# LoRA add on one core: the two-tile part of the output stored in four uneven pieces from two queues

## The chip, the cores and the metric

The kernel runs on one core of one Trainium2 chip. The metric is the device time of one execution in microseconds; lower is better. The core has a matmul engine (PE; its weight loads are shown apart as PEld), VectorE (DVE), ScalarE (ACT), GpSimd (POOL) and SyncE (SP). Data moves between HBM and the on-chip memory by 16 DMA engines, which all queues share. SyncE issues every transfer of the kernel before.

## The reference

```
x: (16, 512, 768) float32    A: (768, 16)    B: (16, 768)    scale: 0.5
lora = np.matmul(np.matmul(x, A), B)
return (x + scale * lora).astype(np.float32)
```

Flattened, x has 8192 rows of 768 numbers, 25.17 MB. As much is written, so 50.3 MB cross the DMA engines at least once.

## The kernel before

The 8192 rows are 64 tiles of 128 rows. All of x stays in one on-chip buffer `xs`, 128 partitions by 64 tiles by 768 numbers, and the result is added in place there, so a store reads what a load wrote.

Loads and stores go in parts, with a layout of their own: in a part of n tiles, partition p holds n consecutive rows of x. One partition's share of a part is therefore one run of n x 3072 bytes in HBM, and a DMA packet of the profile is one such run. `PARTS` (line 14) lists parts of 2, 6, 8, 16, 16 and 16 tiles; `LOADS` splits the first part of 16 into two loads of 8. A transfer of a part has 128 partition rows, 8 for each of the 16 DMA engines: 6,144 bytes a row for two tiles, 24,576 for eight, 49,152 for sixteen.

SyncE issues in this order: the loads of 2 and 6 tiles, A (24 rows of 2,048 bytes), B (16 rows of 3,072 bytes), the other loads, and then the stores in the order `STORES = [2, 1, 0, 3, 4, 5]`: the parts of 8, 6 and 2 tiles, then three of 16. Ahead of a store it waits on the semaphore `added`, on which VectorE counts finished parts (line 158). All this stands in one queue, and each DMA engine works off its share of that queue in order. The two-tile part is part 0, the third store.

The computing goes by chunks of four tiles. VectorE and ScalarE cast x to fp16 (`narrowed`, lines 99 and 101), the PE transposes it (line 193), ScalarE copies the transposed block out (line 143), the PE multiplies by A (line 201), ScalarE scales (line 147), the PE multiplies by B (line 212), and VectorE adds the result to `xs` (`summed`, line 154). The PE's program is a loop (`Fori`) over the chunks; the other engines' programs are unrolled.

GpSimd zeroes a scratch area and builds the identity matrix in the first two microseconds, and then waits at line 132 until `stored` has counted all six stores (16 each). That wait is the last thing it does before the closing barriers, and it is what keeps the kernel open until the output has landed. A wait is carried by the next instruction of its engine, here the branch out of the block that the loop ends.

Of the kernel before, what the change touches and what calls it, by code (L numbers as in the profile page):

```python
# [13 lines left out]
PARTS = [2, 6, 8, 16, 16, 16]  # L14
LOADS = [2, 6, 8, 8, 8, 16, 16]
STORES = [2, 1, 0, 3, 4, 5]

CHUNK = 4

# [2 lines left out]
def kernel(  # L22
# [8 lines left out]
    nc = tc.nc  # L31
    fp32 = mybir.dt.float32
    add = mybir.AluOpType.add
    P = 128

    x2 = x.flatten_outer_dims()
    out2 = out.flatten_outer_dims()
# [8 lines left out]
    NB = D // 32  # L46
    assert D % W == 0 and sum(LOADS) == NT == sum(PARTS) and sorted(STORES) == list(range(len(PARTS)))
    n_splits = [(n0, min(512, D - n0)) for n0 in range(0, D, 512)]
# [5 lines left out]
    xs = sb.tile([P, NT, D], fp32, name="xs")  # L54
# [17 lines left out]
    starts = [sum(PARTS[:i]) for i in range(len(PARTS))]  # L72

    def rows(t2, t0, n):
        i = max(i for i in range(len(PARTS)) if starts[i] <= t0)
        part = t2[ds(starts[i] * P, PARTS[i] * P), :].rearrange("(p s) d -> p s d", s=PARTS[i])
        return part[:, ds(t0 - starts[i], n), :]

    with tc.tile_critical():  # L79
        names = "zeroed ident a b a_t prep fed0 fed1 fed2 turned got proj y lora freed added".split()  # L80
        S = {k: nc.alloc_semaphore(name=f"s_{k}") for k in names}
        landed = [nc.alloc_semaphore(name=f"s_load{i}") for i in range(len(LOADS))]
        stored = nc.alloc_semaphore(name="s_stored")
        part_of = [i for i, n in enumerate(LOADS) for _ in range(n)]

        def load(i):
            t0, n = sum(LOADS[:i]), LOADS[i]
            nc.sync.dma_start(out=xs[:, t0 : t0 + n, :], in_=rows(x2, t0, n)).then_inc(landed[i], 16)
# [3 lines left out]
        def narrowed(engine, c, u):  # L92
# [16 lines left out]
            out=ident, in_=ident, compare_op=mybir.AluOpType.not_equal, fill=1.0,  # L109
# [8 lines left out]
            out=a_rows[0:NB, :, :], in_=A.rearrange("(b a) r -> b a r", a=32)  # L118
# [3 lines left out]
            load(i)  # L122
        nc.sync.wait_ge(S["prep"], 1)
        load(len(LOADS) - 1)
        summed_parts = 0
        for i in STORES:
            t0, n = starts[i], PARTS[i]
            if i + 1 > summed_parts:
                summed_parts = i + 1
                nc.sync.wait_ge(S["added"], summed_parts)  # L130
            nc.sync.dma_start(
                out=rows(out2, t0, n), in_=xs[:, t0 : t0 + n, :]
            ).then_inc(stored, 16)
        nc.gpsimd.wait_ge(stored, 16 * len(STORES))


        nc.scalar.wait_ge(S["ident"], 1)
# [2 lines left out]
        for c in range(NC):  # L140
# [3 lines left out]
            if c + 1 < NC:  # L144
# [3 lines left out]
                out=yt, in_=yt_ps, func=mybir.ActivationFunctionType.Copy, scale=sc  # L148
# [89 lines left out]
            expanded(s)  # L238


# [1 line left out]
_INS = ['x', 'A', 'B', 'scale']  # L242
_OUTS = [((16, 512, 768), 'float32')]
# [30 lines left out]
```

## Time and profile before

| | |
|---|---|
| median of 3 runs | 125.21 us (125.16 to 125.56) |
| the profiled execution's own time | 125.21 us |
| its span, first to last instruction | 123.4 us |
| PE / VectorE / ScalarE / GpSimd busy | 83.9 / 80.3 / 76.5 / 1.2 us |
| bytes moved | 50.45 MB at 409 GB/s |
| last store issued (SP) | 102.65 us |

The span leaves 1.8 us of the execution's time outside. The page cuts the span in 40 slices and gives a digit for each engine in each (its busy share in tenths); it also counts the DMA packets by size. Each transfer ends, on each DMA engine that it used, with one small packet of 4 bytes that counts up the transfer's semaphore. The kernel has no other packets under 512 bytes, so such a packet in a window of time tells that one engine has come to the end of its share of one transfer.

### The profile page before, as it was taken

Reading aid. Unit: us, or ns where it says so; the run is one execution under the profiler, and the core shown is the slowest. Engines: PE = TensorE matmul, PEld = TensorE weight load, DVE = VectorE, ACT = ScalarE, POOL = GpSimd, SP = SyncE. Lnnn points to the kernel's source line nnn. Section 1 sums busy time; section 2 is a strip of 40 time slices with the busy share of each in tenths; the row PEclk is TensorE's granted clock in tenths of the full one; section 3 lists DMA queues with packets and bytes.
Section 4 is the critical chain, followed back from the end, with each engine's and each line's share of the span. In section 5 each row is a group of like instructions: output and inputs, shape, how many; then the busy total and the mean of one; then the engine's idle time right before and its main releaser. Section 6 shows DMA issues by size and latency. Waiting matters only on the chain. (4 is left out here: it accounts for less than half of the span.)

```text
span 123.4 us, 1795 instructions
## 1 busy us (share of the span) xinstructions
PE 83.9 (68%) x608; PEld 39.2 (32%) x608; DVE 80.3 (65%) x102; ACT 76.5 (62%) x130; POOL 1.2 (1%) x7
## 2 busy tenths in 40 slices
PE   0000499999999999999999999999999770000000
PEld 0000343445444454444444444444444200000000
DVE  0002932999999999999999999989997592000000
ACT  4002539889898898988989889898898400000000
POOL 3000000000000000000000000000000000000000
PEclk9999999999999999999999999999999955555555
DMA  3999999999999799989799999989989989997960
GB/s 86 444 460 372 438 398 470 406 406 486 398 510 478 303 496 494 430 353 494 271 462 406 414 460 500 466 350 478 446 350 478 478 382 414 494 462 335 494 287 0
DMA packets 1942, 50.45 MB, mean 409 GB/s; under 512 B 236, under 2 KB 236, under 8 KB 532
## 3 DMA queue, kind: packets, MB, share of 16 engines
q1 hardware_dynamic: 1940, 50.43, 95.9%
q14 instruction: 2, 0.02, 0.0%
HBM read 25.26 MB, written 25.17 MB: 409 GB/s over the span
## 5 line engine op out<-in xcount | busy, mean ns | idle before, releaser
L154 DVE TENSOR_TENSOR xs<-xs,lo_ps 128x768 f32<-128x768 f32 x64 | 58.2, 950 | 5.9 <-PE lo_ps L212 5.1
L143 ACT CAST xt<-xt_ps 128x512 f16<-128x512 f32 x96 | 52.4, 577 | 10.5 <-PE xt_ps L193 8.8
L193 PE MATMUL xt_ps<-ident,xh 128*128 128x128 f16 x384 | 33.8, 226 | 12.3 <-PEq L186 12.3
L201 PE MATMUL yt_ps<-xt,a_mm 128*16 128x512 f16 x96 | 32.6, 395 | 1.6 <-PEq L186 1.6
L101 DVE CAST xh<-xs 128x1024 f16<-128x1024 f32 x32 | 21.9, 688 | 16.4 <-DMA xs<-in_x_dram 11.5
L193 PEld LDWEIGHTS xt_ps<-ident,xh 128*128 128x128 f16 x384 | 22.5, 100 | 30.4 <-issue 30.4
L212 PE MATMUL lo_ps<-b_mm,yt 16*128 16x512 f16 (+1 forms) x128 | 27.2, 331 | 3.7 <-PEq L186 1.6
L99 ACT CAST xh<-xs 128x1024 f16<-128x1024 f32 x16 | 16.8, 1048 | 9.1 <-DMA xs<-in_x_dram 9.1
L212 PEld LDWEIGHTS lo_ps<-b_mm,yt 16*128 16x128 f16 x128 | 9.6, 92 | 13.6 <-issue 7.6
L201 PEld LDWEIGHTS yt_ps<-xt,a_mm 128*16 128x16 f16 x96 | 7.1, 86 | 17.7 <-issue 12.7
L147 ACT ACTIVATE yt<-yt_ps 16x512 f16<-16x512 f32 x16 | 9.4, 587 | 0.9 <-PE yt_ps L201 0.9
L138 ACT ACT_TABLE_LOAD x1 | 1.3, 1283 | 0.9 <-SPq L79 0.9
L166 DVE STREAM_TRANSPOSE xs<-xs 32x512 f32<-32x512 f32 x1 | 1.0, 1027 | 0.0
L170 DVE CAST a_mm<-xs 32x96 f16<-32x96 f32 x4 | 0.9, 231 | 0.1
L172 DVE CAST b_mm<-xs 16x768 f16<-16x768 f32 x1 | 0.5, 549 | 0.0
L105 POOL MEMSET xs<- 32x512 f32 x1 | 0.5, 514 | 0.5 <-SPq L79 0.5
L108 POOL TENSOR_SCALAR_AFFINE_SELECT ident<-ident 128x128 f16<-128x128 f16 x1 | 0.3, 294 | 0.2 <-POOL ident L106 0.2
L138 ACT COPY first<-ident 128x1 f16<-128x1 f16 x1 | 0.2, 193 | 0.0
L106 POOL MEMSET ident<- 128x128 f16 x1 | 0.2, 194 | 0.0
L255 POOL MEMSET const-uint8-127<- 128x1 uint8 x1 | 0.1, 103 | 0.0
L255 POOL MEMSET const-bfloat16-1.0<- 128x1 bf16 x1 | 0.1, 102 | 0.0
L255 POOL MEMSET const-float32-0.0<- 128x1 f32 x1 | 0.1, 99 | 0.2 <-issue 0.2
(1 smaller groups left out, 0.1 us busy)
## 6 DMA issues: line engine op xcount, KB each, us to landing
out_dram<-xs SPq DMA_DIRECT2D x3, 6144.0 KB, 25.2
xs<-in_x_dram SPq DMA_DIRECT2D x2, 6144.0 KB, 45.9
xs<-in_x_dram SPq DMA_DIRECT2D x3, 3072.0 KB, 22.8
out_dram<-xs SPq DMA_DIRECT2D x1, 3072.0 KB, 29.3
xs<-in_x_dram SPq DMA_DIRECT2D x1, 2304.0 KB, 10.0
out_dram<-xs SPq DMA_DIRECT2D x1, 2304.0 KB, 34.4
xs<-in_x_dram SPq DMA_DIRECT2D x1, 768.0 KB, 4.5
out_dram<-xs SPq DMA_DIRECT2D x1, 768.0 KB, 35.7
```

The lines of the kernel that those rows point to most:

```text
L99: i = engine.copy(out=xh[u], in_=src)
L101: i = engine.tensor_copy(out=xh[u], in_=src)
L105: nc.gpsimd.memset(a_rows, 0.0).then_inc(S["zeroed"], 1)
L138: nc.scalar.copy(out=first, in_=ident[:, 0:1])
L143: nc.scalar.copy(out=xt[j], in_=xt_ps[j % NX]).then_inc(S["got"], 1)
L147: nc.scalar.activation(out=yt, in_=yt_ps, func=mybir.ActivationFunctionType.Copy, scale=sc).then_inc(S["y"], 1)
L154: nc.vector.tensor_tensor(out=xs[:, k, :], in0=xs[:, k, :], in1=lo_ps[k % 2], op=add).then_inc(S["freed"], 1)
L166: nc.vector.transpose(out=a_t, in_=a_rows.rearrange("b a r -> b r a")).then_inc(S["a_t"], 1)
L170: nc.vector.tensor_copy(out=a_mm[ds(32 * k, 32), :, :], in_=a_tv[:, k, :, :])
L193: i = nc.tensor.matmul(xt_ps[j % NX][:, ds(s * P, P)], xh[u][:, s, ds(h * P, P)], ident, start=True, stop=True,)
L201: i = nc.tensor.matmul(yt_ps, a_mm[:, j, :], xt[j], start=(j == 0), stop=(j == ND - 1))
L212: i = nc.tensor.matmul(lo_ps[s % 2][:, ds(n0, w)], yt[:, ds(s * P, P)], b_mm[:, ds(n0, w)], start=True, stop=True,)
```

## The change

Part 0, the two-tile part, is no longer one store of 128 partition rows. GpSimd stores partitions 0 to 4 and 5 to 103 (5 and 99 rows), on a queue of its own and with a semaphore of its own for each; SyncE stores partitions 104 to 119 and 120 to 127 (16 and 8 rows) in the place where the whole part stood. GpSimd issues its two pieces when part 0 has been added and the last load has landed, waits for both to land, and then runs `dma_reset` over the two semaphores, which in the built program is a drain instruction. Its wait for SyncE's stores, now seven (5 whole parts and 2 pieces), stands after the PE's loop in the program, that is on the branch of the next block. The instructions of the PE, VectorE and ScalarE and their order are the same.

```
+UNEVEN = 0
...
+        apart = [nc.alloc_semaphore(name=f"s_apart{k}") for k in range(2)]
...
+        def store(engine, i, p0, p, done):
+            t0, n = starts[i], PARTS[i]
+            engine.dma_start(
+                out=rows(out2, t0, n)[ds(p0, p)], in_=xs[ds(p0, p), t0 : t0 + n, :]
+            ).then_inc(done, 16)
+        uneven = [(nc.gpsimd, 5), (nc.gpsimd, 99), (nc.sync, 16), (nc.sync, 8)]
+        begins = [sum(p for _, p in uneven[:k]) for k in range(len(uneven))]
         summed_parts = 0
         for i in STORES:
-            t0, n = starts[i], PARTS[i]
             if i + 1 > summed_parts:
                 summed_parts = i + 1
                 nc.sync.wait_ge(S["added"], summed_parts)
-            nc.sync.dma_start(
-                out=rows(out2, t0, n), in_=xs[:, t0 : t0 + n, :]
-            ).then_inc(stored, 16)
-        nc.gpsimd.wait_ge(stored, 16 * len(STORES))
+            if i != UNEVEN:
+                store(nc.sync, i, 0, P, stored)
+                continue
+            for (engine, p), p0 in zip(uneven, begins):
+                if engine is nc.sync:
+                    store(engine, i, p0, p, stored)
+        nc.gpsimd.wait_ge(S["added"], UNEVEN + 1)
+        nc.gpsimd.wait_ge(landed[-1], 16)
+        pool = [(p, p0) for (engine, p), p0 in zip(uneven, begins) if engine is nc.gpsimd]
+        for (p, p0), done in zip(pool, apart):
+            store(nc.gpsimd, UNEVEN, p0, p, done)
+        for done in apart:
+            nc.gpsimd.wait_ge(done, 16)
+        nc.gpsimd.dma_reset(range(apart[0].num, apart[-1].num + 1))
+        n_sync = len(STORES) - 1 + len(uneven) - len(pool)
...
         for s in range(CHUNK):
             expanded(s)
+        nc.gpsimd.wait_ge(stored, 16 * n_sync)
```

## The prediction

> **What bounds the kernel now.** I read the page first: spans, slices, queues.
>
> ```profile
> span 123.4 us, 1795 instructions
> PE 83.9 (68%) x608; PEld 39.2 (32%) x608; DVE 80.3 (65%) x102; ACT 76.5 (62%) x130; POOL 1.2 (1%) x7
> ...
> DVE  0002932999999999999999999989997592000000
> ...
> DMA  3999999999999799989799999989989989997960
> ...
> DMA packets 1942, 50.45 MB, mean 409 GB/s; under 512 B 236, under 2 KB 236, under 8 KB 532
> q1 hardware_dynamic: 1940, 50.43, 95.9%
> q14 instruction: 2, 0.02, 0.0%
> ```
>
> No computing engine is busy in the last six slices; the DMA engines are nearly full from the first slice to the last but one. The transfers set the time. The store rows, and the chain of waits, say how much room computing has:
>
> ```profile
> L131 SPq DMA_DIRECT2D out_dram<-xs x6: 332/340/433, 41.5 to 102.6; - x6
> DMA to landing us min/median/max: 19.7/30.1/35.7
> ```
>
> ```profile
> 100.75 1.82 DVE xs L154 x2
> ```
>
> VectorE's last add ends at 102.57, the last store is issued at 102.65 and lands 19.7 us later, at 122.35. That store is 8 rows an engine. The packet view from 45.35 to 45.36 holds one 49,152-byte packet at 1134.4% of 16 x 0.01 us, 1.815 us; eight take 14.5 us. The first engines end it near 119.95 (below), so they began it at 105.4, 2.8 us after its issue. Some of that is an issue's own time: the first load is issued at 0.95 and nothing moves before 2.0. Late computing has a cover of about 1.7 us.
>
> Then I asked the packet view for the stretch in which the last store ends, window by window, for its completion packets (the ones under 512 B). The windows, in order: 119.8 to 120.1, 120.2 to 120.8, 121.2 to 121.3, 121.8 to 122.0.
>
> ```profile
> DMA packets 11, 0.05 MB, mean 164 GB/s; under 512 B 10, under 2 KB 10, under 8 KB 10
> ...
> DMA packets 4, 0.00 MB, mean 0 GB/s; under 512 B 4, under 2 KB 4, under 8 KB 4
> ...
> DMA packets 1, 0.00 MB, mean 0 GB/s; under 512 B 1, under 2 KB 1, under 8 KB 1
> ...
> DMA packets 1, 0.00 MB, mean 0 GB/s; under 512 B 1, under 2 KB 1, under 8 KB 1
> ```
>
> Ten engines end by 120.1. Of the four, narrower windows put two at 120.34 to 120.39 and two at 120.68 to 120.70. One ends near 121.25 (call it Z) and the last near 121.9 (W). The kernel waits for W alone. The mean of the sixteen is (10 x 119.95 + 2 x 120.36 + 2 x 120.69 + 121.25 + 121.9) / 16 = 120.28: moving rows between engines can gain at most 1.6 us.
>
> The end of the last load (61.7 to 62.0, 62.2 to 62.7, 63.1 to 63.22) shows the same spread without W: 11, 4 and 1 engines.
>
> ```profile
> DMA packets 22, 0.27 MB, mean 901 GB/s; under 512 B 11, under 2 KB 11, under 8 KB 11
> ...
> DMA packets 11, 0.17 MB, mean 344 GB/s; under 512 B 4, under 2 KB 4, under 8 KB 4
> ...
> DMA packets 4, 0.07 MB, mean 614 GB/s; under 512 B 1, under 2 KB 1, under 8 KB 1
> ```
>
> So Z is late by the loads, and W falls back during the stores. A cause for such a loss shows at 45.0 to 45.1: an instruction-loading packet on one engine,
>
> ```profile
> q14 instruction: 1, 0.01, 19.9%
> ```
>
> which is 0.32 us (19.9% of 1.6), and the data packet that starts behind it, at 45.36 to 45.38, takes 686.9% of 0.32 = 2.20 us instead of 1.815. A second such pair stands at 54.2 and 54.55 (2.48 us).
>
> **The change part by part.**
>
> *Rows between engines.* A row of the two-tile part costs 0.234 us: the window 76.0 to 76.3 holds 21 such packets at 102.4% of 4.8 us. Before, each engine has 8. How does a transfer with fewer rows spread? The page counts 236 completion packets; 14 transfers with 16 or 128 rows make 224, which leaves 12 for the 24 rows of A: 12 engines, two rows each, the largest divisor up to 16. By that, 5 rows go to 5 engines, 99 to 11 engines with 9 each, 16 to all, 8 to 8. As 5 + 11 = 16, the two GpSimd pieces can fill disjoint sets. If the 8 rows cover the five, these carry 1 + 1 + 1 = 3 rows, three others 9 + 1 + 1 = 11, eight others 10 (together 128). The five gain 5 x 0.234 = 1.17 us, the others lose 0.47 or 0.70.
>
> No view says which engines W and Z are. Both bounds of this term: with W and Z among the five, W ends at 121.9 - 1.17 = 120.73 and Z at 120.08; the engines at 120.69 then set the end, at 121.16 or 121.39 (at 120.8 to 121.1 if they are among the five too). That is -0.5 to -1.1 us. With W among the rest, +0.47 to +0.70. I take -0.74 (end at 121.16): the one kind of loss that the rows show, instruction loading, falls on single engines, as W's and Z's lateness does, and a fixed group of a few engines is where such losses would repeat. This is the weakest choice of the sum.
>
> [...] The trace agrees with the divisor for A's 24 rows; no view here numbers the engines. [...]
>
> *The second queue.* From about 64 us on the engines have work from GpSimd's queue beside SyncE's. The trace of before has no GpSimd transfer. Lower bound: nothing, bytes are the same. Upper bound: each change of queue costs what the instruction packet costs its neighbour, 0.38 us; nine rows on an engine, 3.4 us. The loads' and stores' own row changes cost nothing (94 packets from 109 to 119.8 keep 98.7% busy), and these are the nearer row, being plain data; I take +0.1.
>
> [...]
>
> *Completion packets.* Up to three more on an engine at some 0.01 us each (120.34 to 120.39: 2 packets, 2.2% of 0.8 us = 0.018): +0.03 at most.
>
> *SyncE.* Two issues instead of one, +0.43 us by the slowest issue row, at about 42.4. It next waits for VectorE until 62.1: hidden; without that cover it would be 0.43 us on the next store's issue, which itself queues for 10 us.
>
> *GpSimd.* New waits for `added`, the last load (its last completion packet at 63.2, and 0.45 us more to land if W's 121.9 to 122.35 is a guide) and its own landings. Behind them on GpSimd stands only the drain and the last wait; nobody waits for GpSimd until 122. How long it takes to issue is unknown. Nearest rows: 0.43 us for an issue, 9 to 36 us to land in a full queue. Even 36 us on top of 64 ends at 100, 20 us before it matters. If GpSimd's writing slows VectorE's adds, the 1.7 us of cover above hold it, and beyond that each microsecond counts.
>
> *The last wait.* Between W's landing at 122.35 and the end of the span 1.05 us pass with some ten steps; one branch leaves them. Bounds 0 and -0.2 (two average steps); I take -0.05.
>
> Sum against the profiled execution (125.21, equal to the median): -0.74 + 0.1 + 0.03 - 0.05 = -0.66: 124.55.
>
> **The rivals.**
>
> *Rows pile onto the late engines* (slower). Place: the two-tile store. If GpSimd's pieces take sixteen engines in even shares, seven rows each until 99 are gone, then fourteen engines get 7, one gets 1, one none; with the 5, 16 and 8 rows on the first engines, five carry 10 rows, three 9, six 8, and two only 2 and 1. W and Z as the last two would gain (-1.1, ending by 120.85 at the engine with two more rows); W among the first eight ends 1 or 2 rows later, +0.23 or +0.47, and with divisors but W outside the five, +0.47 to +0.70. It decides from the first row above 8 on W. 125.4 to 125.9, centre 125.65. For: nothing in the trace ties the five to W. Against: Z and W carry most of the lateness, and losses that belong to a group of engines would be met by a group.
> [...]
>
> *Queue changes cost* (slower): 0.1 to 0.38 us for each of nine or ten rows on eleven engines, 1 to 3.4 us, less the 0.7: 125.5 to 128, centre 126.2. For: 0.38 and 0.66 us beside instruction packets. Against: those happen on another kind of traffic.
>
> *Nothing comes of it*: W's lateness is made after 63 us and may shift to another engine when rows move, or W gets exactly 8 rows: 125.0 to 125.4. For: W was not late at 62. Against: three runs within 0.4 us.
>
> **How the numbers follow.** Forecast 0.48, its own range 124.1 to 124.9; pile-up 0.28; queue changes 0.12; nothing 0.12. A measurement of this kernel tells 0.3%, 0.38 us, from no change: 124.83 and 125.59. Faster: 0.44 of the forecast and 0.04 of the pile-up case (W and Z as the emptied two): 0.48. Same: 0.04 of the forecast, 0.08 of the pile-up, 0.10 of nothing: 0.22. Slower: 0.16 of the pile-up, 0.12 of queue changes, 0.02 of nothing: 0.30. The range, 124.1 to 126.0, leaves out most of the queue changes and the ends of the rest.
>
> **What would show it.** Right: after, the last store's completion packets stand within 1.3 us of one another instead of 2; the last at about 121.1; a GpSimd queue with 104 packets of 6,144 bytes. Its completion count tells the spreading: 16 for divisors (5 + 11), more for even shares. Wrong: W's packet at 122.1 or later (pile-up), or the first ten packets also later by over 0.7 us (queue changes). A last store that is issued after 106 would show VectorE slowed beyond its cover.

## The result, and the profile after

The changed kernel takes 125.82 us (median of 7 runs, 125.61 to 125.99) against 125.20 us (7 runs, 125.10 to 125.56). The ratio is 1.0048, 95% interval 1.0035 to 1.0062: slower by about 0.6 us. The profiled execution took 125.99 us, a little over its median, with a span of 124.2 us.

From the page of the changed kernel: span, the DMA row of the 40 slices, packet counts, and the queues with packets, MB and share of 16 engines' time.

```profile
span 124.2 us, 1801 instructions
...
DMA  3999999999999979989989899989999998999970
...
DMA packets 2006, 50.45 MB, mean 406 GB/s; under 512 B 300, under 2 KB 300, under 8 KB 596
...
q1 hardware_dynamic: 1844, 49.79, 94.6%
q0 software_dynamic: 160, 0.64, 1.4%
```

The bytes are the same. GpSimd's queue (q0) has 160 packets for 104 rows: 56 small ones, where two transfers with one completion packet on each of 16 engines would need 32. 160 is 16 x (7 + 1 + 1 + 1): every engine got seven packets for the 99 rows and one for the 5, and a completion packet for each of the two transfers. An engine that had no row left got a 4-byte packet in its place: 16 x 7 - 99 = 13 for the long piece and 16 - 5 = 11 for the short one, 24 in all, and 32 + 24 = 56. So the 99 rows go in even shares of 7, rounded up, and not by the largest divisor: with shares filled in order, fourteen engines get 7 rows, one gets 1, one none. The trace has them so: from 70.5 to 75.6 us this queue's 4-byte packets stand in two series, 0.69 us apart, one of seven and one of six ahead of their completion packets.

The store rows (least, median and longest issue in ns; first and last start):

```profile
L129 SPq DMA_DIRECT2D out_dram<-xs x7: 322/351/432, 42.0 to 103.0; - x7
L129 POOL DMA_DIRECT2D out_dram<-xs x2: 612/634/656, 64.5 to 65.2; - x2
...
DMA to landing us min/median/max: 6.4/9.7/13.1
```

GpSimd issues in 0.63 us each and its pieces land within 13.1 us, by 78.3, far ahead of the end. The last store goes out at 103.0 instead of 102.65, with the cover of the prediction still there.

The end, again by the completion packets of the last store. Windows 119.8 to 120.9, 120.9 to 121.6, 121.9 to 122.2, 122.6 to 122.8:

```profile
DMA packets 13, 0.20 MB, mean 179 GB/s; under 512 B 9, under 2 KB 9, under 8 KB 9
...
DMA packets 3, 0.00 MB, mean 0 GB/s; under 512 B 3, under 2 KB 3, under 8 KB 3
...
DMA packets 3, 0.00 MB, mean 0 GB/s; under 512 B 3, under 2 KB 3, under 8 KB 3
...
DMA packets 1, 0.00 MB, mean 0 GB/s; under 512 B 1, under 2 KB 1, under 8 KB 1
```

The last engine ends near 122.7 instead of 121.9, and four engines end after 121.6, where only W did before: the spread has grown, not shrunk. One more thing is new. Windows just wide enough for one packet, at 76.266 to 76.270 and 76.394 to 76.396, hold a single row of 6,144 bytes each:

```profile
q1 hardware_dynamic: 1, 0.01, 2393.8%
...
q1 hardware_dynamic: 1, 0.01, 4737.5%
```

2393.8% of 16 x 0.004 us is 1.53 us, 4737.5% of 16 x 0.002 is 1.52 us, for packets that take 0.234 us before. These are rows of SyncE's pieces. Two theories stood after this: *rows* (the engine that ends last got two rows more) and *second queue* (taking turns between two queues lengthens packets).

### The profile page after: what moved, and what is told of

The parts are those of the page before. It is cut to its first block, busy times and chain, and to the rows that moved or that the text cites. A ratio compares the mean times of both kernels' runs of the same rounds, so it can differ in the third digit from the quotient of the medians.

```text
span 124.2 us, 1801 instructions
## 1 busy us (share of the span) xinstructions
PE 84.2 (68%) x608; PEld 39.7 (32%) x608; DVE 80.3 (65%) x102; ACT 76.5 (62%) x130; POOL 2.4 (2%) x9
## 5 line engine op out<-in xcount | busy, mean ns | idle before, releaser
L215 PE MATMUL xt_ps<-ident,xh 128*128 128x128 f16 x384 | 34.4, 229 | 12.3 <-PEq L208 12.3
L215 PEld LDWEIGHTS xt_ps<-ident,xh 128*128 128x128 f16 x384 | 23.0, 102 | 30.4 <-issue 30.4
L129 POOL DMA_DIRECT2D out_dram<-xs x2 | 1.3, 634 | 62.4 <-DMA xs<-in_x_dram 62.4
## 6 DMA issues: line engine op xcount, KB each, us to landing
out_dram<-xs POOLq DMA_DIRECT2D x1, 594.0 KB, 13.1
```

Source lines behind the costliest of these rows:

```text
L129: engine.dma_start(out=rows(out2, t0, n)[ds(p0, p)], in_=xs[ds(p0, p), t0 : t0 + n, :]).then_inc(done, 16)
L215: i = nc.tensor.matmul(xt_ps[j % NX][:, ds(s * P, P)], xh[u][:, s, ds(h * P, P)], ident, start=True, stop=True,)
```

## The experiments

All are edits of the changed kernel's list of pieces, unless said otherwise; where GpSimd has no piece, its issues, waits and drain go too. Each was timed beside the kernel before on the same chip, and the ratios are to that kernel.

**One piece by GpSimd.**

```
+        uneven = [(nc.gpsimd, 128)]
```

> GpSimd stores all 128 rows of the two-tile part in one piece; SyncE stores none of them. Every DMA engine keeps 8 rows. Theory rows (the +0.62 us of the change is two more rows of 0.234 us on the engine that ends last, and little else): 125.2 to 125.35, and the last completion packet again near 121.9. Theory second queue (turns between two queues lengthen packets on all engines; the changed kernel had packets of 1.5 to 2.6 us at 75 to 78 us): 125.5 to 126.0. Packets of GpSimd's queue: 16 x (8 + 1) = 144 if the shares are even.

Measured: 125.20 us, ratio 0.9997 (0.9988 to 1.0006). GpSimd's queue in the stretch from 69 to 79.5:

```profile
q0 software_dynamic: 140, 0.76, 17.4%
```

17.4% of 16 x 10.5 us is 29.2 us for 124 rows (0.76 MB) and some marks, 0.235 us a row. A second queue, GpSimd's issue, its waits and the drain together cost nothing that can be told from none. The second-queue theory falls.

**SyncE alone, 112 + 16 rows.**

```
+        uneven = [(nc.sync, 112), (nc.sync, 16)]
```

> SyncE alone stores the part, in 112 and 16 rows: 7 + 1 rows on every engine, no GpSimd transfer. Theory rows: 125.2, as before (8 rows an engine). Theory second queue: also 125.2. Third theory, short pieces (a SyncE transfer with one row an engine leaves the engine waiting for what comes next): 125.4 to 125.8, with long packets near 75 to 78 us.

Measured: 126.28 us, ratio 1.0080 (1.0053 to 1.0106), single runs from 125.3 to 126.6. The median is above the ranges of all three theories. Every engine has as many rows as before, and yet this is slower than the change itself. Rows alone don't explain it; something in the pieces does.

**SyncE alone, 104 + 24 and 88 + 40 rows.**

```
+        uneven = [(nc.sync, 104), (nc.sync, 24)]
```

> SyncE alone, 104 and 24 rows. By the largest divisor up to 16 these use 13 and 12 engines with 8 and 2 rows: twelve engines carry 10 rows, one 8, three none, as many on the fullest engines as in the changed kernel, without GpSimd. Theory rows: the engine that ends last is among the twelve, +0.47: 125.6 to 125.75, and packets at the end spread as after. Theory second queue: 125.2. Short pieces: at most +0.3 (two rows an engine).

```
+        uneven = [(nc.sync, 88), (nc.sync, 40)]
```

> SyncE alone, 88 and 40 rows: 11 engines with 8 rows, 10 with 4 more; ten engines carry 12 rows, one 8, five none. Theory rows: twice the dose of the 104 and 24 case, +0.94 us: 126.05 to 126.25, if the engine that ends last is one of the ten. Theory second queue and short pieces: 125.2 to 125.4.

Measured: 125.66 us, ratio 1.0034 (1.0021 to 1.0047), and 126.13 us, 1.0076 (1.0063 to 1.0089). Between the two lie two rows on the fullest engines and 0.47 us, as two rows of 0.234 us would make. The two profiled executions lie only 0.28 us apart (125.73 and 126.01), so this agreement of the medians is no exact price. The spread by divisors shows at the end. In the window 118 to 119.3 the kernel before has no completion packet; here, 104 + 24 first, then 88 + 40:

```profile
DMA packets 13, 0.49 MB, mean 378 GB/s; under 512 B 3, under 2 KB 3, under 8 KB 3
```

```profile
DMA packets 16, 0.54 MB, mean 416 GB/s; under 512 B 5, under 2 KB 5, under 8 KB 5
```

Three engines and five engines finish early, as many as were to get no row. So SyncE's rows are spread as the divisor has it in these two runs (13 and 11 engines); GpSimd's 99, by the 160 packets, are not.

**Halves: 64 + 64 rows, and two whole tiles.** A third theory, *memory side*, a guess of the author's: a transfer that covers a part of the partitions makes engines meet at the same place. In the second kernel, part 0 is two transfers of all 128 partitions, one a tile.

```
+        uneven = [(nc.sync, 64), (nc.sync, 64)]
```

> SyncE alone stores the two-tile part as partitions 0 to 63 and 64 to 127: 4 + 4 rows on every engine, as many rows as before, no piece shorter than 4 rows an engine. In the runs with 112 + 16, 104 + 24 and 88 + 40 rows single 6,144-byte packets took up to 1.1 us. Theory memory side (a transfer of all 128 partitions gives each engine partitions of its own, a transfer of a part of them makes engines meet at the same place of the on-chip memory, so packets slow down though rows are equal): the strongest case, sixteen engines in one half at a time; up to 8 x 0.234 = 1.9 us more: 126.0 to 127.1, with the 6,144-byte packets far above 0.234 us on average. Theory short pieces (an engine that gets one row waits for what comes next): 125.2 to 125.3.

```
-            nc.sync.dma_start(
-                out=rows(out2, t0, n), in_=xs[:, t0 : t0 + n, :]
-            ).then_inc(stored, 16)
+            for t in (range(t0, t0 + n) if i == 0 else (t0,)):
+                m = 1 if i == 0 else n
+                nc.sync.dma_start(
+                    out=rows(out2, t, m), in_=xs[:, t : t + m, :]
+                ).then_inc(stored, 16)
```

> SyncE alone stores the two-tile part as two transfers of one tile each, all 128 partitions, 3,072 bytes a row: also one transfer more, 8 short rows an engine each, but every transfer covers all partitions. Memory side: 125.2 to 125.35 (16 packets of 0.121 us instead of 8 of 0.234 are +0.06). Any theory in which one more store on SyncE's queue, or shorter packets, cost: 125.5 and above.

Measured: 125.58 us, ratio 1.0035 (1.0021 to 1.0048), for the halves, and 125.25 us, 1.0006 (0.9997 to 1.0015), for the tiles. One more transfer and shorter packets cost nothing that can be told from none (1.0006); splitting by partitions does cost (1.0035), with no row moved and no piece under four rows an engine. The direction was as the theory had it; the size, +0.39 us, was half of the least that it gave.

**The clash on a long transfer.** From here on, *clash* is the name for this slowing of packets in a transfer of a part of the partitions. The same halves on the last part of 16 tiles (`UNEVEN = 5`), the two-tile part whole.

> The last part of 16 tiles (49,152 bytes a row) is stored by SyncE as partitions 0 to 63 and 64 to 127, the two-tile part whole; 8 rows an engine everywhere. If half of the partitions can be read only at half the rate for as long as the transfer lasts, the last store takes up to twice its 14.5 us: 132 to 139. If the clash costs a fixed time for each packet or transfer (0.4 to 0.9 us on single packets of the two-tile runs), 125.4 to 126.5.

Measured: 138.30 us, ratio 1.1048 (1.1031 to 1.1065). In two stretches of the last store (columns: length; busy time of the five engines; granted clock, DMA share, GB/s), first this kernel, then the kernel before:

```profile
106.00:112.00 6.00, 0.00 (x0) 0.00 (x0) 0.00 (x0) 0.00 (x0) 0.00 (x0) 0.50 0.98 221
112.00:118.00 6.00, 0.00 (x0) 0.00 (x0) 0.00 (x0) 0.00 (x0) 0.00 (x0) 0.50 0.99 213
```

```profile
106.00:112.00 6.00, 0.00 (x0) 0.00 (x0) 0.00 (x0) 0.00 (x0) 0.00 (x0) 0.50 0.95 410
112.00:118.00 6.00, 0.00 (x0) 0.00 (x0) 0.00 (x0) 0.00 (x0) 0.00 (x0) 0.50 0.93 401
```

The engines are shown as busy, at little over half the rate. This is far above what a fixed time for each packet or transfer was to cost (126.5 at most): in these stretches half of the partitions gave about half of the bandwidth, 221 and 213 GB/s against 410 and 401. No run here separates the on-chip side from the HBM side, so the place of the clash and what makes it are guessed and not shown.

**Both queues, rows even.**

```
+        uneven = [(nc.gpsimd, 112), (nc.sync, 16)]
```

> GpSimd stores 112 rows, SyncE 16: 7 + 1 rows on every engine, as in the 112 + 16 case of SyncE alone (126.28), with a second queue. Memory side: 125.4 to 126.5, long packets of both queues near 70 to 78 us. Rows alone: 125.2. If it comes out clearly under the SyncE-only case, the spread over time that the second queue brings softens the clash.

Measured: 125.34 us, ratio 1.0013 (1.0004 to 1.0022). This is taken for the clash without a shift of rows, on the queues of the change: some 0.15 us, a little under the least that the theory gave and far under the 1.03 us of the same sizes from SyncE alone.

**One row more.**

```
+        uneven = [(nc.gpsimd, 104), (nc.sync, 24)]
```

> GpSimd 104 rows in one piece, SyncE 24. With even shares on GpSimd (7 rows on fourteen engines, 6 on one) and divisors on SyncE (2 rows on twelve) the engine that ends last carries 9 rows, one more than before and one less than in the changed kernel. Sum from the earlier runs: +0.15 (112 + 16 on the same two queues) + 0.234 = 125.2 + 0.38 = 125.6. GpSimd packets: 16 x (7 + 1) = 128. If GpSimd used divisors (13 engines, 8 rows): 208 less or more, 104 + 13 or 104 + 16 packets, and 10 rows: 125.8.

Measured: 125.52 us, ratio 1.0027 (1.0017 to 1.0036), +0.31 us against the 0.38 of the sum. The GpSimd packets are 128, as even shares give:

```profile
q0 software_dynamic: 128, 0.64, 1.3%
```

**Which engine ends last.**

```
+        uneven = [(nc.sync, 88), (nc.sync, 35), (nc.sync, 5)]
```

> SyncE alone, 88, 35 and 5 rows: 11, 7 and 5 engines; rows per engine 14 on the first five, 13 on the next two, 8 on four, none on five. Rows: six more rows on the engine that ends last, +1.40, if it is one of the first five: 126.6 to 126.9 with the clash; +1.17 if it is one of the next two; if it is none of the seven, the end is set by other engines, 125.4 to 126.0.

Measured: 126.84 us, ratio 1.0135 (1.0120 to 1.0151), +1.63 us. Six rows and a clash like the 0.15 make 1.55; five rows, for the next two engines, would make 1.32. That alone would leave the engine open, but the trace settles it.

In the traces of the kernel before and the changed one, a packet nearly always begins 3 or 4 ns before the packet ahead of it on its engine ends, so an engine's packets can be followed back from its last one. W then has a mark of its own. In the kernel before, its store packets are longer than the other engines' from 63.6 to 103.8 us: 0.95 to 0.99 us instead of 0.912 for 24,576 bytes, and 1.85 to 1.95 instead of 1.815 for 49,152, some 2 us in all. One of them, in the window 82.929 to 82.933:

```profile
q1 hardware_dynamic: 1, 0.05, 2990.6%
```

2990.6% of 16 x 0.004 us is 1.914 us. The changed kernel has one engine with this mark too, from 63.7 to 104.6 us, and so have the other runs that are followed back here. In the run with 88 + 35 + 5 rows the five engines with 14 rows are the last five to end, and the marked one is among them: it ends at 123.34, 1.44 us later than before, close to the 1.40 of six rows. So W is one of the five engines that every piece fills. The kernel's end, 123.64, is another of the five; its rows were lengthened by 2.3 us in all.

**The same pieces in the other order.**

```
+        uneven = [(nc.sync, 16), (nc.sync, 112)]
```

> SyncE alone, as the 112 + 16 run (126.28, from 125.3 to 126.6), the 16 rows first: partitions 0 to 15 and 16 to 127. Memory side: the clash moves to other engines; 125.3 to 126.6, long 6,144-byte packets again. Short pieces at the end of the part: back to 125.2.

Measured: 125.37 us, ratio 1.0013 (1.0004 to 1.0022), against 1.0080 for 112 + 16. The same two sizes cost 0.16 or 1.0 us. In these two runs, what the clash costs hangs on whether an engine that is late already is hit. Followed back in the two traces, W ends at 121.97 in both. The engine that ends the kernel is one whose loads ended late (63.2 and 63.7 us, as Z's in the kernel before): with 112 + 16 its rows were lengthened by 1.7 us and it ends at 123.12, with 16 + 112 by 0.4 us, and it ends at 122.17. One of its rows with 112 + 16, in the window 78.6 to 78.604, took 0.79 us (1232.8% of 16 x 0.004):

```profile
q1 hardware_dynamic: 1, 0.01, 1232.8%
```

**The last wait alone.** The kernel before, with only that line moved:

```
-        nc.gpsimd.wait_ge(stored, 16 * len(STORES))
...
         for s in range(CHUNK):
             expanded(s)
+        nc.gpsimd.wait_ge(stored, 16 * len(STORES))
```

> The kernel before with only GpSimd's last wait put behind the PE's loop; all stores as before. All theories: 125.1 to 125.25; the prediction had it at -0.05, bounds 0 and -0.2. The time from the last store's landing to the end of the span falls from 1.05 us to about 1.0.

Measured: 125.21 us, ratio 1.0002 (0.9993 to 1.0011). No effect that can be told from none. From the last completion packet to the end of the span 1.52 us pass in this trace, as many as in the kernel before and in the changed one.

No version was found that beats the kernel before; the whole piece by GpSimd and the two tiles equal it.

## Why the prediction was wrong

*What bounds the kernel* held: the transfers set the time, and within them one engine, W. (The mean of the sixteen ends is 120.30, not 120.28; nothing hangs on it.) The row price held (0.234 forecast, 0.235 in GpSimd's whole piece). Nothing in the runs speaks against the small terms for SyncE's extra issue and the completion packets, and GpSimd's pieces landed long before the end, as forecast.

*Rows between engines* is the step that failed. It carried the divisor, read from SyncE's transfer of A, over to GpSimd's two pieces, and let five engines, W among them, lose five rows: -0.74. GpSimd's queue counts 160 packets, even shares. Five engines then carry 1 + 7 + 1 + 1 = 10 rows, and W, which the 88 + 35 + 5 run puts among them, gains two: +0.47 by the row price. The trace of the changed kernel shows it directly. Followed back from 122.69, the last engine has W's mark and ten rows: one and seven from GpSimd, two from SyncE. Five engines have ten rows, and the one whose loads ended last is among them too. So the choice that the prediction called its weakest, W and Z among the five, was right; wrong was the number of rows that this gave them. The prediction had this as its first rival, at +0.47 for these engines, with the even shares as a supposition that nothing before showed; GpSimd's 160 packets show them for 99 rows, and the 128 of the later run for 104. The centre of that rival was 125.65, and its sign, W's packet at 122.1 or later, is what came.

*The second queue* was priced by the wrong mechanism. Its +0.1 stood for turns between queues, which cost nothing that can be told from none (one piece by GpSimd, 0.9997). What the pieces do cost is the clash, longer packets where a transfer covers a part of the partitions, which no term and no rival of the prediction named: about 0.15 us in the 112 + 16 run on both queues. In the profiled execution of the changed kernel, W's ten rows took 2.83 us, where eight took 1.97 before. Of the 0.86 us between, 0.47 are the two rows and 0.39 are longer packets, above all SyncE's two rows, in the windows 77.222 to 77.226 and 77.613 to 77.617:

```profile
q1 hardware_dynamic: 1, 0.01, 606.2%
...
q1 hardware_dynamic: 1, 0.01, 756.2%
```

That is 0.39 and 0.48 us instead of 0.234.

*The last wait*: -0.05 forecast, nothing measured.

The sum of what was measured alone is 0.47 + 0.15 = 0.62 us, and the change cost 0.62 us. The 0.15 has an interval from 0.05 to 0.28 us, the clash hits different engines in different splits, and the profiled execution, 0.17 us over the median, has 0.39 in its place (0.86 in W's rows, of which 0.78 are left at its end, 122.69 against 121.90). So the closeness is partly luck. The two engines that were left with 1 and 2 rows could not have ended the kernel earlier in any case: W was not one of them.

What stays open is why W's packets are longer during the stores, and with it whether it could be helped. In the kernel before they return to the common length at 103.8, soon after VectorE's last add (102.57), but no run tests a connection. By the shares read above, every partial transfer that was tried puts rows on W's group.

## What to carry to other kernels

Before rows are moved between DMA engines, find out which engine ends last and which engines each piece will fill: here the spread differed by issuing queue (99 rows of GpSimd's on 15 engines, 104 and 88 of SyncE's on 13 and 11), and GpSimd's packet count and the engines that ended early told which held. In these runs a cut along the free dimension was the cheaper one: two tiles of all 128 partitions cost nothing that can be told from none for the two-tile part (1.0006), two halves of the partitions 0.39 us; for the last part halves ran at about half rate (213 to 221 GB/s instead of 401 to 410). With the DMA engines evenly full (95.9% of their time in the kernel before), a rearrangement between them could gain no more than the spread at their end, 1.6 us, and longer packets ate into it.

## What the runs showed of the hardware

- GpSimd's two transfers of the change, 5 and 99 rows, had 24 4-byte packets where an engine had no row left, beside 32 for completion: 160 in all, 10 an engine.
- From 106 to 118 us, a store of 64 partitions ran at 213 to 221 GB/s where one of 128 ran at 401 to 410, while the DMA engines were shown 98 to 99% busy (93 to 95% at the higher rate): the busy share did not tell slow packets from fast ones.
- A row of 6,144 bytes took up to 1.53 us instead of 0.234 in the pieces of the change.
- One engine's store packets were some 5% longer than the others' in the kernel before, from 63.6 to 103.8 us (1.914 us against 1.815 for 49,152 bytes), and in the changed one, from 63.7 to 104.6; it ended both.
- Where both queues had work, the last engine of the changed kernel took one data packet of each in turn, from 69.7 to 77.2 us.
